# Mixing stage of a two-block transformer kernel: all transfers but weights and gate vectors issued from the GpSimd queue, gate columns by way of DRAM, head states and decay rows loaded ahead of the projections

## The chip, the cores and the metric

The kernel runs on one core of one Trainium2 chip. The metric is the time that the device takes for one execution, in microseconds, lower being better. A profile of one execution gives the rows that are read below. PE is TensorE (matrix products), DVE is VectorE, ACT is ScalarE, POOL is GpSimd, SP is SyncE, whose queue issues transfers and computes nothing. A name such as L1314 is line 1314 of the kernel before.

## The reference

Two transformer blocks are computed in float32 for one sequence of 512 tokens of width 1024. The first block has a feed-forward layer, a mixing layer and a second feed-forward layer, and beside the 512 tokens a context of 256 tokens goes through the first two. The second block (attention, cross attention to a memory, a feed-forward layer with a convolution) isn't touched here. The mixing layer is what matters:

```python
qk = silu(short_conv(concatenate([q, k]), conv_w, conv_b))      # q, k, v: 4 heads of 256
# for both directions (forward, reverse), per chunk of 128 tokens, per head:
b = cumsum(lf); g = b[-1]; w = g - b + li                        # lf: log forget gate, li: log input gate
m_new = maximum(g + m_st, max(w)); ws = exp(w - m_new); decay = exp(g + m_st - m_new)
c_new = decay * c_st + einsum('sv,sk->vk', v * ws, k)            # the state, passed to the next chunk
dm = b[t] - b[s] + li[s];  m_t = maximum(b + m_st, max(dm))
s_ts = (q @ k.T) * exp(dm - m_t)                                 # only s <= t
inter = exp(b + m_st - m_t)
h = (s_ts @ v + inter * (c_st @ q)) / maximum(|den|, exp(-m_t))
# the context's scan gives only the state that the 512 tokens start from
y_a = sigmoid(o) * head_layernorm(h_fwd + h_rev)
y_b = gelu(u) * spatial_mix(rmsnorm(gelu(vs)))
mixed = sigmoid(ga) * (y_a @ w_a) + sigmoid(gb) * (y_b @ w_b)
out = h + gate * (mixed @ w_out)
```

## The kernel before, in words

**Products.** Every float32 product is made of three: both operands are split into a high and a low part, and `mm3` (L109 to L111) adds high x high, high x low and low x high in one PSUM bank. Weights come in panels of 512 KB: `raw` (L94) loads one into one of three buffers from SP's queue, and `split` (L98 on ACT, L99 on DVE) makes the two parts. `fm` runs a panel against x: 24 products.

**Order.** The program is written once in a plain order. When the kernel is built, a planner lays the instructions of each engine into that engine's queue: what stands earlier in the program goes first, if by the planner's own estimates it is ready at that time; if not, something later is put there. On the chip each queue is then worked off strictly in order. So an instruction that becomes ready later than was estimated holds up everything behind it on its engine. A transfer also stands in the queue of the engine that issues it, and waits there for its source and its destination.

**The mixing stage** (`mix`, L1027) runs through these parts:
- the context's feed-forward layer; with it the norm of the 512 tokens, whose h is stored to DRAM (L1038);
- `lat_in`: gates and the last head's v for the 512 tokens (`cols_in`, v to DRAM at L1213); then `sgu`, whose u loop also makes the context's gates (`ctx_in`);
- the gate chain (`ctx_prep`, `lat_prep`): the gates as rows [4 heads, tokens], moved with small transfers (L1248, L1249), running sums by scans on DVE (L1253, L1266), exponentials on ACT; `decay_bc` (L1299, L1301) spreads the chunk decays over all partitions by way of DRAM; the rows dI and dM go to DRAM (L1338, L1339); `cols` stacks rows in one SBUF tile (L1311) and PE turns them into columns (L1314);
- the z loop, written behind the gate chain: 8 blocks, each the product of a gate panel with x and of a panel of w_branch_b with y_b;
- the context heads (`ctx_state`, 4 times): k and v of the head with the context's x, k turned token-major (`token_major`, L1395), for both directions two chunks of `state_update`, and the state to DRAM (L1430);
- the latent heads (4 times): `head_proj` makes k, q, v and o; `head_core` turns k, loads the states (L1440), makes the scores q k (L1445), loads for each direction a dM row (L1450, into a shared temporary) and a dI row (L1452), each spread over 128 partitions, forms P by a subtraction, a minimum, an exponential and a product with the scores (L1455 to L1460) and a triangular select on POOL (L1462); then 4 chunks in both directions with products with the state (L1476) and of P with v (L1477), state updates, and, where both directions of a chunk are there, a layer norm whose reciprocal root is on POOL (L1494) and whose turned output (L1503) is put off;
- the ga loop (gates to DRAM, L1067), the fin loop (gates back, L1075; L1082 loads h again), and the output product.

The last head's v isn't projected but loaded (L1360). Temporaries (`tmp`) share five buffers. All transfers of this stage but the first few small ones go out from SP's queue, between the weight panels. POOL does memsets, the small steps of the norms, the selects and the reciprocal roots.

Of the kernel before, what the change touches and what calls it, by code (L numbers as in the profile page):

```python
# [9 lines left out]
F32 = mybir.dt.float32  # L10
# [4 lines left out]
P = 128  # L15
D = 1024
KD = D // P
S = 512
# [7 lines left out]
class Core:  # L26
    def __init__(self, ctx, tc):
# [20 lines left out]
        nc.vector.tensor_copy(self.ones, one)  # L48
        self.mhalf = self.const.tile([P, 1], F32, name="mhalf")
# [7 lines left out]
    def flush(self, keep=0):  # L57
        """issues what was put off (but the last `keep`) so that products in between hide its wait"""
        while len(self.late) > keep:
            self.late.pop(0)()  # L60
# [23 lines left out]
    def spare(self, src, k):  # L84
        """like raw, in the space that the gate takes later"""
# [47 lines left out]
    def mean(self, ss, n, add=EPS, tag="s1"):  # L133
        """ss / n + add"""
# [4 lines left out]
    def power(self, m):  # L139
        """m ** -0.5"""  # L140
        rs = self.small()
        self.nc.gpsimd.tensor_tensor(out=rs, in0=m, in1=self.mhalf, op=ALU.pow)
        return rs
# [16 lines left out]
    def norm_tile(self, src, rs, A, B, out, t, banks=None):  # L160
        """src: the two halves [128 tok, 512]; out (hi, lo) [128, 8, N]; columns t*128.. are written."""
# [6 lines left out]
    def norm_steps(self, src, A, B, out, ts, step=None):  # L168
        """steps that norm the token tiles ts; src(t) gives the two halves."""
# [39 lines left out]
    def ranges(self, items, x, ranges, at=1):  # L209
        """items: (weights, psum); all of one token range come before the next range. What was put off is issued  # L210
        within the first range, after item `at`."""
# [5 lines left out]
    def ffn_pair(self, fs, w_in, x, ranges, n=S, w=None):  # L217
        """The two products of the tiles fs."""
# [13 lines left out]
    def ffn_in(self, pool, w_in, x, start, each, finish, w0=None):  # L232
        """start: tiles taken together while the last token tiles of x are still on their way."""
# [11 lines left out]
    def tm_out(self, act, w, kt, evac, post=None, ts=range(NT), tail=0, tail0=0, bk=range(NT), first=0):  # L245
        """act: list of (hi, lo) [128, 512] per contraction tile; w [kt*128, 1024]; evac(t, half, psum).
        In the second half the last panels are taken token tile by token tile, so post(t, half) can follow early."""
# [27 lines left out]
    def gate(self, i):  # L275
        """gate i with the vector along every row"""
# [31 lines left out]
def body(ctx, tc, a, out):  # L308
# [14 lines left out]
    with tc.tile_pool(name="start", bufs=1) as stp:  # L323
        def ada_pe(v, hf, parts):
            """steps for half a vector, one weight panel each. parts: 1: weights and conditions as they are;
            2: both as hi and lo."""
# [116 lines left out]
    def ada_dve(v, srcs):  # L443
        """queues the products for one vector; each piece is one weight panel. The sum over partitions: within
        blocks of 32 by transposes on DVE, then over the four blocks by a product that puts them in place."""
# [10 lines left out]
        def along_rows(hf, st):  # L456
            """the sums over partitions, on every row"""
# [97 lines left out]
def norm_post(K, h, A, B, g=None, bk=range(NT), store=None):  # L555
    """post(t, half) for tm_out: the norm of h as hi and lo. With g, h is first replaced by rmsnorm(h, g), and goes to `store`."""
# [50 lines left out]
def attention(K, a, h_d, cC, x, km_d, vm_d):  # L607
# [5 lines left out]
    with ExitStack() as sc:  # L613
# [7 lines left out]
        def queries(off, early=()):  # L621
            """the four panels of columns that start at off, for all tokens"""
# [8 lines left out]
        def proj_v(v, off, extra=None):  # L631
            """extra: [128, 4, n] for the n columns of w_in that follow v"""
# [12 lines left out]
        def proj_fox():  # L645
            """q has the high and the low part of a head in the two halves of the partitions, k the high part in both"""
# [22 lines left out]
        def pv(p, n, dst, copy=nc.vector.tensor_copy):  # L669
            """dst: per 128-block of p the (out, rhs, start, stop) of its product."""  # L670
# [9 lines left out]
        def pipeline(items):  # L680
            """items: generators; a stage of one item is issued together with earlier stages of the next ones."""
# [160 lines left out]
def memory_kv(K, a, src, rs, g, pool, km_d, vm_d, banks):  # L842
    """the keys and values of the memory, to DRAM; returns its steps, one weight panel each."""
# [31 lines left out]
def memory_attention(K, a, h, cC, x, km_d, vm_d, mp):  # L875
# [6 lines left out]
    def load(hd):  # L882
        """the head's keys and values"""
# [6 lines left out]
    def parts(hd):  # L890
        """the same in two parts each"""
# [22 lines left out]
    def weights(hd):  # L914
        """softmax over the memory for all tokens"""
# [113 lines left out]
def mix(K, a, h, xc, mods, affine, g_mix, g_head, g_sgu, g_ffn2, conv_w, conv_b):  # L1029
    nc, tc = K.nc, K.tc  # L1030
    w_in = a["w_in"][0]
    with ExitStack() as sc:
# [5 lines left out]
        K.bg.append(lambda: nc.sync.dma_start(out=hd_, in_=h))  # L1038
# [4 lines left out]
        with ExitStack() as sx:  # L1043
# [9 lines left out]
            with tc.tile_pool(name="ck", bufs=1) as ck:  # L1053
                for hd in range(NH):
# [503 lines left out]
```

## Time and profile before

| what | value |
|---|---|
| median of 3 runs | 2528.09 us (2526.84 to 2533.28) |
| span of the profiled execution | 2527.8 us |
| PE busy | 2451.1 us, 97% |
| DVE busy | 1358.2 us, 54% |
| ACT busy | 1012.5 us, 40% |
| POOL busy | 120.4 us, 5% |
| mean granted PE clock | 0.987 |
| share of 16 DMA engines' time, SP's queue | 43.3% |
| transfers issued by POOL | none |

The profiled execution's own time is its span, 2527.8 us from the first to the last instruction; no other time lies around it in the figures here, and it is 0.3 us under the median. Busy time is the union of an engine's instructions. Products on PE overlap, so PE can be busy and yet run at half the clock; the clock is read from the column PEclk, where 1.00 is 2.4 GHz and 0.50 is 1.2 GHz.

### The profile page before, as it was taken

To read this page: it belongs to the slowest core of one execution; us is meant where nothing else is said; L and a number is where in the kernel's file an instruction comes from. 1 tells how busy PE (TensorE), PEld (TensorE's weight loads), DVE (VectorE), ACT (ScalarE), POOL (GpSimd) and SP (SyncE) were. 2 spreads that over 40 slices of the span, in tenths; PEclk is the share of its full clock that TensorE was granted. 3 is DMA by queue.
4 is the path that set the end of the run, shared out by engine and by line. 5 is a ranking of instruction groups with operands and counts; after the bars stand their busy time and mean duration, and the time that the engine had idled before them with its cause. 6 is when DMAs were issued, how large, how long until landed. Compare 5 with 4: busy or idle time off the path is not lost.

```text
span 2527.8 us, 32182 instructions
## 1 busy us (share of the span) xinstructions
PE 2451.1 (97%) x12538; PEld 2040.3 (81%) x12538; DVE 1358.2 (54%) x2106; ACT 1012.5 (40%) x1685; POOL 120.4 (5%) x261
## 2 busy tenths in 40 slices
PE   8999999999999899999899999999999999999998
PEld 5778888899887688887688888888777788888887
DVE  5778755465445355566545333235485464666632
ACT  5533232354354344344234322224475453544422
POOL 2000000000010000000001000001020100000000
PEclk9999999999999999999999999999999999999999
DMA  8667654565754475454443333223213231333221
GB/s 266 218 188 218 181 167 159 171 185 185 172 81 97 78 138 138 79 87 78 84 161 111 108 98 94 100 92 110 75 29 106 76 117 50 107 95 101 94 99 67
DMA packets 373498, 307.09 MB, mean 121 GB/s; under 512 B 10579, under 2 KB 311043, under 8 KB 372833
## 3 DMA queue, kind: packets, MB, share of 16 engines
q1 hardware_dynamic: 371201, 301.35, 43.3%
q10 hardware_dynamic: 2144, 3.67, 0.4%
q8 instruction: 99, 1.62, 0.3%
q14 instruction: 54, 0.44, 0.1%
HBM read 291.43 MB, written 13.44 MB: 121 GB/s over the span
## 4 chain that ended last, share of the span: by engine, by line
PE 83%; DMA 6%; DVE 4%; issue 4%; ACT 2%; POOL 1%; SPq 0%; POOLq 0%; ACTq 0%; DVEq 0%
PE p L109 25%; PE p L110 25%; PE p L111 25%; DMA raw<-in_w_in_dram 2%; DMA tmp<-dM 2%; PE p L678 1%; DVE wl L99 1%; PE p L198 1%; ACT wh L98 1%; DMA gtmp<-gtmp 1%; PE p L673 1%; PE p L747 1%; PE p L1476 1%; PE p L1477 1%; DMA raw<-in_w_mkv_dram 0%
## 5 line engine op out<-in xcount | busy, mean ns | idle before, releaser
L99 DVE TENSOR_TENSOR wl<-raw,wh 128x1024 fp32r<-128x1024 f32 (+2 forms) x447 | 543.6, 1218 | 714.6 <-ACT wh L98 692.3
L98 ACT CAST wh<-raw 128x1024 fp32r<-128x1024 f32 (+2 forms) x447 | 466.7, 1046 | 942.1 <-PE p L110 371.9
L109 PE MATMUL p<-xh,wh 128*128 128x512 f32 (+1 forms) x1728 | 609.8, 353 | 3.8 <-ACT wh L98 2.3
L110 PE MATMUL p<-xl,wh 128*128 128x512 f32 (+1 forms) x1728 | 608.7, 353 | 0.6 <-DVE xl L207 0.6
L111 PE MATMUL p<-xh,wl 128*128 128x512 f32 (+1 forms) x1728 | 608.3, 352 | 0.0
L109 PEld LDWEIGHTS p<-xh,wh 128*128 128x128 f32 x1728 | 326.6, 189 | 48.9 <-ACT wh L98 2.7
L110 PEld LDWEIGHTS p<-xl,wh 128*128 128x128 f32 x1728 | 327.0, 189 | 45.2 <-DVE xl L207 1.0
L111 PEld LDWEIGHTS p<-xh,wl 128*128 128x128 f32 x1728 | 326.8, 189 | 43.9
L109 PE MATMUL p<-wh,ah 128*128 128x512 f32 x616 | 243.2, 395 | 0.5 <-ACT ah L98 0.5
L111 PE MATMUL p<-wh,al 128*128 128x512 f32 x616 | 242.7, 394 | 0.3 <-DVE al L99 0.3
L110 PE MATMUL p<-wl,ah 128*128 128x512 f32 x616 | 242.7, 394 | 0.0
L110 PE MATMUL p<-mxl,wh 128*128 128x512 f32 x384 | 155.9, 406 | 0.0
L111 PE MATMUL p<-mxh,wl 128*128 128x512 f32 x384 | 155.0, 404 | 0.0
L109 PE MATMUL p<-mxh,wh 128*128 128x512 f32 x384 | 154.6, 403 | 0.0
L111 PEld LDWEIGHTS p<-wh,al 128*128 128x128 f32 x616 | 115.9, 188 | 27.6 <-DVE al L99 0.8
L109 PEld LDWEIGHTS p<-wh,ah 128*128 128x128 f32 x616 | 116.0, 188 | 26.6 <-ACT ah L98 0.9
L110 PEld LDWEIGHTS p<-wl,ah 128*128 128x128 f32 x616 | 116.0, 188 | 25.5
L229 DVE TENSOR_TENSOR tmp<-tmp,p 128x512 f32<-128x512 f32 (+1 forms) x66 | 39.4, 597 | 96.4 <-PE p L111 94.4
L111 PEld LDWEIGHTS p<-mxh,wl 128*128 128x128 f32 x384 | 73.7, 192 | 16.8
L110 PEld LDWEIGHTS p<-mxl,wh 128*128 128x128 f32 x384 | 74.2, 193 | 15.8
L109 PEld LDWEIGHTS p<-mxh,wh 128*128 128x128 f32 x384 | 73.8, 192 | 15.8
L98 ACT CAST ah<-tmp 128x512 fp32r<-128x512 f32 (+1 forms) x88 | 49.8, 566 | 84.3 <-DVE tmp L1004 55.8
(422 smaller groups left out, 3578.6 us busy)
## 6 DMA issues: line engine op xcount, KB each, us to landing
raw<-in_w_ffn_in_dram SPq DMA_DIRECT2D x132, 512.0 KB
raw<-in_w_in_dram SPq DMA_DIRECT2D x98, 512.0 KB
raw<-in_w_ffn_out_dram SPq DMA_DIRECT2D x66, 512.0 KB
raw<-in_w_ada_dram SPq DMA_DIRECT2D x53, 512.0 KB
raw<-in_w_up_dram SPq DMA_DIRECT2D x44, 512.0 KB
raw<-in_w_down_dram SPq DMA_DIRECT2D x22, 512.0 KB
raw<-in_w_mkv_dram SPq DMA_DIRECT2D x16, 512.0 KB
raw<-in_w_out_dram SPq DMA_DIRECT2D x16, 512.0 KB
```

The lines of the kernel that those rows point to most:

```text
L98: self.nc.scalar.copy(hi, src)
L99: self.nc.vector.tensor_tensor(out=lo, in0=src, in1=hi.bitcast(F32), op=ALU.subtract)
L109: mm(out, ah, bh, start=start, stop=False)
L110: mm(out, ah, bl, start=False, stop=False)
L111: mm(out, al, bh, start=False, stop=stop)
L198: nc.tensor.transpose(ps[:, k * P:(k + 1) * P], hn[:, k * P:(k + 1) * P], self.ident)
L229: nc.vector.tensor_tensor(out=pr, in0=sa, in1=b, op=ALU.mult)
L673: nc.tensor.transpose(pt[:, j * P:(j + 1) * P], p[:, j * P:(j + 1) * P], K.ident)
L678: nc.tensor.matmul(out, pT[:, j * P:(j + 1) * P], rhs, start=start, stop=stop)
L747: nc.tensor.matmul(ps[:, b * L:(b + 1) * L], sq[p0:p0 + DH, c, i * P:L], sk[p0:p0 + DH, c, :L], start=True, stop=True)
L1476: nc.tensor.matmul(X, qi[:, j], C[d][:, j], start=j == 0, stop=False)
L1477: nc.tensor.matmul(X, Pm[d][:, c], T["v"][:, c, :HD + 1], start=False, stop=True)
```

## The change

`K.side_dma` is the issue of a transfer from POOL. In the mixing stage every transfer except weight panels, the gate vector and a few small loads of other queues now uses it. `stack` writes the gate rows to DRAM instead of one SBUF tile; `cols` loads them from there, and is called later in the program: the context's columns behind the first context head's k and v, the latent ones behind the last context state. `ctx_state` is split: `ctx_kv` of the next head stands ahead of the state updates of this one. `head_loads`, called first in `head_proj`, loads both states, both dM rows and both dI rows of a head; the dM tile (one buffer for each direction) is worked on in place until it is P. No arithmetic is added or left out. Doc strings are also dropped (not shown).

```diff
@@ class Core
+        self.side_dma = nc.gpsimd.dma_start
@@ mix
-        K.bg.append(lambda: nc.sync.dma_start(out=hd_, in_=h))
+        K.bg.append(lambda: K.side_dma(out=hd_, in_=h))
...
             with tc.tile_pool(name="ck", bufs=1) as ck:
+                kv = ctx_kv(K, ck, 0, xg, w_in, conv_w, conv_b, v_d[1])
+                G.ctx_cols()
                 for hd in range(NH):
-                    ctx_state(K, ck, hd, xg, w_in, conv_w, conv_b, G, C_d, v_d[1])
+                    nxt = ctx_kv(K, ck, hd + 1, xg, w_in, conv_w, conv_b, v_d[1]) if hd + 1 < NH else None
+                    ctx_state(K, ck, hd, kv, G, C_d)
+                    kv = nxt
+                G.lat_cols()
...
-                T = head_proj(K, hp, hd, x, w_in, conv_w, conv_b, v_d[0])
+                T = head_proj(K, hp, hd, x, w_in, conv_w, conv_b, v_d[0], G, C_d)
...
-                nc.sync.dma_start(out=ga_d[:, d], in_=ga)
+                K.side_dma(out=ga_d[:, d], in_=ga)
...
-                nc.sync.dma_start(out=ga, in_=ga_d[:, d])
+                K.side_dma(out=ga, in_=ga_d[:, d])
...
-            nc.sync.dma_start(out=h, in_=hd_)
+            K.side_dma(out=h, in_=hd_)
@@ class Gates
-            nc.sync.dma_start(out=v_d[:, t], in_=v)
+            K.side_dma(out=v_d[:, t], in_=v)
...
-            nc.sync.dma_start(out=LI, in_=g[8 * d:8 * d + 4, :])
-            nc.sync.dma_start(out=LF, in_=lf[8 * d + 4:8 * d + 8, :])
+            K.side_dma(out=LI, in_=g[8 * d:8 * d + 4, :])
+            K.side_dma(out=LF, in_=lf[8 * d + 4:8 * d + 8, :])
...
-            nc.sync.dma_start(out=dd[4 * d:4 * d + 4, :], in_=res[d]["decay"])
+            K.side_dma(out=dd[4 * d:4 * d + 4, :], in_=res[d]["decay"])
...
+    def ctx_cols(self):
+        self.ccols = self.cols(self.cstack, 2, "ctx")
+
+    def lat_cols(self):
+        self.lcols = self.cols(self.lstack, 4, "lat")
+
+    def stack(self, stacks, nch, name):
+        K = self.K
         n = nch * P
         r = len(stacks) * 4
-        st = self.tmp()[:r, :n]
+        st = K.dram.tile([r, n], F32, name=name + "_stack")
         for i, s in enumerate(stacks):
-            nc.sync.dma_start(out=st[4 * i:4 * i + 4, :], in_=s)
+            K.side_dma(out=st[4 * i:4 * i + 4, :], in_=s)
+        return st
+
+    def cols(self, st, nch, name):
+        K, nc = self.K, self.K.nc
+        r = st.shape[0]
+        rows = K.tmp()[:r, :nch * P]
+        K.side_dma(out=rows, in_=st)
+        st = rows
         ps = K.psB()
...
-        self.ccols = self.cols([res[0]["w"], res[1]["w"]], 2, "ctx")
+        self.cstack = self.stack([res[0]["w"], res[1]["w"]], 2, "ctx")
...
-            nc.sync.dma_start(out=self.dI[d], in_=it)
-            nc.sync.dma_start(out=self.dM[d], in_=r["M"])
+            K.side_dma(out=self.dI[d], in_=it)
+            K.side_dma(out=self.dM[d], in_=r["M"])
...
-        self.lcols = self.cols([res[0]["g"], res[1]["g"], res[0]["w"], res[1]["w"], floor[0], floor[1]], 4, "lat")
+        self.lstack = self.stack([res[0]["g"], res[1]["g"], res[0]["w"], res[1]["w"], floor[0], floor[1]], 4, "lat")
@@ head_v
-        nc.sync.dma_start(out=dst[:, :, 0:HD], in_=v_d)
+        K.side_dma(out=dst[:, :, 0:HD], in_=v_d)
@@ new, and head_proj
+def head_loads(K, hp, hd, G, C_d, T):
+    T["C"], T["mb"], T["ib"] = [], [], []
+    for d in range(2):
+        t = hp.tile([P, 2, HD + 1], F32, tag=f"C{d}", name="C", bufs=2)
+        K.side_dma(out=t.rearrange("p a b -> p (a b)"), in_=C_d[hd, d])
+        T["C"].append(t)
+        for n, src in (("mb", G.dM), ("ib", G.dI)):
+            t = hp.tile([P, S], F32, tag=f"{n}{d}", name=n)
+            K.side_dma(out=t, in_=src[d, hd].rearrange("(o n) -> o n", o=1).to_broadcast([P, S]))
+            T[n].append(t)
+
-def head_proj(K, hp, hd, x, w_in, conv_w, conv_b, v_d):
+def head_proj(K, hp, hd, x, w_in, conv_w, conv_b, v_d, G, C_d):
     nc = K.nc
     T = {}
+    head_loads(K, hp, hd, G, C_d, T)
@@ ctx_state
-def ctx_state(K, ck, hd, x, w_in, conv_w, conv_b, G, C_d, v_d):
-    nc = K.nc
+def ctx_kv(K, ck, hd, x, w_in, conv_w, conv_b, v_d):
     k = ck.tile([P, 2, NC], F32, tag="k", name="kc", bufs=2)
...
+    return k, v
+
+
+def ctx_state(K, ck, hd, kv, G, C_d):
+    k, v = kv
...
-        nc.sync.dma_start(out=C_d[hd, d], in_=C.rearrange("p a b -> p (a b)"))
+        K.side_dma(out=C_d[hd, d], in_=C.rearrange("p a b -> p (a b)"))
@@ head_core
-    C = []
-    for d in range(2):
-        t = hp.tile([P, 2, HD + 1], F32, tag=f"C{d}", name="C", bufs=2)
-        nc.sync.dma_start(out=t.rearrange("p a b -> p (a b)"), in_=C_d[hd, d])
-        C.append(t)
+    C, mbs, ib = (T[n] for n in ("C", "mb", "ib"))
...
-        mb = K.tmp()
-        nc.sync.dma_start(out=mb, in_=G.dM[d, hd].rearrange("(o n) -> o n", o=1).to_broadcast([P, S]))
-        t = hp.tile([P, S], F32, tag=f"ib{d}", name="ib")
-        nc.sync.dma_start(out=t, in_=G.dI[d, hd].rearrange("(o n) -> o n", o=1).to_broadcast([P, S]))
-        ib.append(t)
-        e = K.tmp().rearrange("p (c t) -> p c t", c=4)
+        pm = e = mbs[d].rearrange("p (c t) -> p c t", c=4)
         nc.vector.tensor_tensor(out=e, in0=G.lcols[:, :, 4 * d + hd:4 * d + hd + 1].to_broadcast([P, 4, P]),
-                                in1=mb.rearrange("p (c t) -> p c t", c=4), op=ALU.subtract)
+                                in1=e, op=ALU.subtract)
...
-        pm = hp.tile([P, 4, P], F32, tag=f"P{d}", name="P")
```

## Rows read from the trace of the kernel before

**Rows 1.** The page, busy time, share of the span and instructions of PE.
```profile
PE 2451.1 (97%) x12538; PEld 2040.3 (81%) x12538; DVE 1358.2 (54%) x2106; ACT 1012.5 (40%) x1685; POOL 120.4 (5%) x261
```
**Rows 2.** Busy time by stretch: engines in us, PEclk, DMA share, GB/s.
```profile
core 0: us, PE busy (x) PEld busy (x) DVE busy (x) ACT busy (x) POOL busy (x), PEclk, DMA share, GB/s
905.00:965.00 60.00, 54.17 (x386) 50.60 (x385) 41.36 (x77) 27.85 (x48) 0.20 (x2) 0.94 0.73 147
1151.00:1162.00 11.00, 7.48 (x25) 5.83 (x24) 6.63 (x16) 3.28 (x6) 1.39 (x2) 0.69 0.22 47
785.00:1250.00 465.00, 424.89 (x2241) 358.26 (x2240) 261.92 (x583) 184.10 (x280) 16.70 (x36) 0.95 0.51 95
```
**Rows 3.** What PE waited for from 785 to 1250: total us, times, longest.
```profile
PE p L1314 <- DMA gtmp<-gtmp: 14.7, 2, 10.6
PE p L1477 <- POOL P L1462: 13.1, 3, 8.6
PE p L1395 <- ACT kc L1353: 3.7, 2, 2.0
PE p L109 <- DVE kT L99: 2.3, 1, 2.3
PE p L109 <- ACT kTc L98: 2.1, 2, 1.8
...
PE p L1476 <- DVE kT L99: 1.9, 1, 1.9
```
**Rows 4.** Busy time by stretch, six stretches behind stalls of PE.
```profile
807.00:813.00 6.00, 6.00 (x16) 4.72 (x17) 1.89 (x3) 0.00 (x0) 0.51 (x1) 0.50 0.33 92
849.60:853.90 4.30, 4.30 (x13) 3.48 (x14) 0.26 (x1) 0.00 (x0) 0.15 (x2) 0.50 0.65 99
940.70:946.00 5.30, 4.94 (x22) 4.65 (x23) 3.77 (x5) 3.42 (x6) 0.00 (x0) 0.50 0.83 178
1007.60:1010.90 3.30, 3.30 (x11) 2.65 (x11) 2.46 (x7) 0.51 (x1) 1.23 (x2) 0.50 0.64 79
...
1155.30:1161.10 5.80, 5.80 (x15) 4.76 (x16) 3.62 (x10) 1.93 (x4) 0.63 (x1) 0.50 0.24 50
1220.30:1225.90 5.60, 5.60 (x15) 4.57 (x16) 3.61 (x10) 1.95 (x4) 0.63 (x1) 0.50 0.22 32
```
**Rows 5.** Timeline of PE, z loop: start us, length us, line, operation.
```profile
809.88 0.63 PE L109 MATMUL p<-ybh,wh 128*128 128x512 f32 x1
810.31 0.63 PE L110 MATMUL p<-ybl,wh 128*128 128x512 f32 x1
810.74 0.63 PE L111 MATMUL p<-ybh,wl 128*128 128x512 f32 x1
...
819.21 0.40 PE L110 MATMUL p<-ybl,wh 128*128 128x512 f32 x1
819.44 0.39 PE L111 MATMUL p<-ybh,wl 128*128 128x512 f32 x1
```
**Rows 6.** The chain of waits from 780 to 1260: start us, us, what.
```profile
934.57 8.28 DMA raw<-in_w_in_dram
...
995.96 8.21 DMA raw<-in_w_in_dram
...
1202.70 14.12 DMA tmp<-dM
```
**Rows 7.** Timeline of SP's queue, context heads and first latent head.
```profile
926.75 6.63 SPq L1430 DMA_DIRECT2D c_store<-Cc  x1
...
981.51 2.98 SPq L1450 DMA_DIRECT2D tmp<-dM  x1
```
**Rows 8.** Timeline of PE, first context head.
```profile
904.29 0.60 PE L1395 MATMUL p<-ident,kc 128*128 128x128 f32 x4
904.64 0.36 PE L109 MATMUL p<-mch,wh 128*128 128x256 f32 x1
```
**Rows 9.** Timeline of POOL, first selects of two latent heads [idle before <-releaser].
```profile
1085.58 0.76 POOL L1462 TENSOR_SCALAR_AFFINE_SELECT P<-P 128x512 f32<-128x512 f32 x1 [51.74 <-DVE P L1460]
...
1219.52 0.70 POOL L1462 TENSOR_SCALAR_AFFINE_SELECT P<-P 128x512 f32<-128x512 f32 x1 [36.45 <-DVE P L1460]
```
**Rows 10.** All instructions with the tensor dM: ns min/median/max, first and last start.
```profile
L1450 SPq DMA_DIRECT2D tmp<-dM x8: 572/2485/4760, 977.6 to 1203.4; - x8
```

More of the change, by code (lines that the diff above doesn't have):

```diff
@@ L1298, in decay_bc @@
         for d in range(2):
-            nc.sync.dma_start(out=dd[4 * d:4 * d + 4, :], in_=res[d]["decay"])
+            K.side_dma(out=dd[4 * d:4 * d + 4, :], in_=res[d]["decay"])
         t = self.pool.tile([P, 8, nch], F32, name=name + "_decay")
-        nc.sync.dma_start(out=t.rearrange("p a b -> p (a b)"), in_=dd.rearrange("a b -> (a b)").rearrange("(o n) -> o n", o=1).to_broadcast([P, 8 * nch]))
+        K.side_dma(out=t.rearrange("p a b -> p (a b)"), in_=dd.rearrange("a b -> (a b)").rearrange("(o n) -> o n", o=1).to_broadcast([P, 8 * nch]))
         return t
-    def cols(self, stacks, nch, name):
-        K, nc = self.K, self.K.nc
+    def ctx_cols(self):
[4 more added lines that the diff above has]
+        K = self.K
         n = nch * P
         r = len(stacks) * 4
-        st = self.tmp()[:r, :n]
+        st = K.dram.tile([r, n], F32, name=name + "_stack")
         for i, s in enumerate(stacks):
-            nc.sync.dma_start(out=st[4 * i:4 * i + 4, :], in_=s)
+            K.side_dma(out=st[4 * i:4 * i + 4, :], in_=s)
[6 more added lines that the diff above has]
+        st = rows
         ps = K.psB()
@@ L1446, in head_core @@
     K.flush()
-    Pm, ib = [], []
+    Pm = []
     for d in range(2):
-        mb = K.tmp()
-        nc.sync.dma_start(out=mb, in_=G.dM[d, hd].rearrange("(o n) -> o n", o=1).to_broadcast([P, S]))
-        t = hp.tile([P, S], F32, tag=f"ib{d}", name="ib")
-        nc.sync.dma_start(out=t, in_=G.dI[d, hd].rearrange("(o n) -> o n", o=1).to_broadcast([P, S]))
-        ib.append(t)
-        e = K.tmp().rearrange("p (c t) -> p c t", c=4)
+        pm = e = mbs[d].rearrange("p (c t) -> p c t", c=4)
         nc.vector.tensor_tensor(out=e, in0=G.lcols[:, :, 4 * d + hd:4 * d + hd + 1].to_broadcast([P, 4, P]),
-                                in1=mb.rearrange("p (c t) -> p c t", c=4), op=ALU.subtract)
+                                in1=e, op=ALU.subtract)
         nc.vector.tensor_scalar(out=e, in0=e, scalar1=0.0, scalar2=None, op0=ALU.min)
         nc.scalar.activation(e, e, AF.Exp)
-        pm = hp.tile([P, 4, P], F32, tag=f"P{d}", name="P")
         nc.vector.scalar_tensor_tensor(out=pm, in0=sps.rearrange("p (c t) -> p c t", c=4), scalar=1.0 / 16.0, in1=e, op0=ALU.mult, op1=ALU.mult)
```

## Prediction, made before the result was known

> **What bounds the kernel now.** I read the page first, then the waits of TensorE (PE), then PE's busy time by stage, and only then the queues. PE is busy 97% of the profiled span [rows 1], so time can be won only where PE stands still or runs slowly. The mixing stage that the change touches holds its gate columns, context heads and latent heads between 785 and 1250 us. There PE is busy 424.89 of 465 us [rows 2], 40.1 us idle; before and after it (the z, branch and output products) I see no wait of PE worth naming, so I cost everything outside at nothing.
>
> The waits of PE in that stretch [rows 3] name the idle time almost wholly: 14.7 us for the gate columns (L1314), 13.1 us for the decay-weighted scores P (L1477), 3.7 us for the context keys (L1395), 2.3 and 1.9 us for latent work, 2.1 us for the context key splits. Behind the longer of them the granted clock stands at 0.50, which is 1.2 GHz instead of 2.4: [rows 4] are the stretches right behind six stalls in which PE is busy at that clock, 6.00, 4.30, 4.94, 3.30, 5.80 and 5.60 us. At full clock one 512-column product starts 0.23 us after the last (819.21, 819.44), at half clock 0.43 us (810.31, 810.74) [rows 5]. So a microsecond of work at half clock gives back 1 - 0.23/0.43 = 0.465 us when the stall before it goes.
>
> Then what is late behind each wait. SP issues weights and everything else in one queue. The chain of waits [rows 6] shows one weight panel landing 8.28 us after its issue, another 8.21 us after, and the last head's dM row 14.12 us after. SP's own row [rows 7]: one store of the context state holds SP for 6.63 us at 926.75 while it waits for VectorE, and the panel that PE then needs goes out only at 934.57 [rows 6]; a dM load holds it 2.98 us at 981.51, and the panel behind it goes out at 995.96 [rows 6].
>
> **The change, part by part.** 84 transfers leave SP's queue for POOL's: 1 store and 1 load of h, 8 stores and 8 loads of the ga gates, 8 and 8 of the context states, 8 dM and 8 dI rows, 6 stores and 2 loads of v, and 26 small gate transfers. Two loads are new (the stacked gate rows come back from DRAM), so POOL issues 86. No product, split or activation is added or removed; PE's work stays the same.
>
> *Gate columns.* Their transposes now stand behind the first context head's products, and behind the last context state. With all of SP's delays PE had both columns' rows by 849.60 [rows 4], and the first context head's products end at 904.29, where its transposes start [rows 8]. So the stores and the load that replace the old transfers have some 50 us of products to hide under. On POOL the transfers stand between the gate chain's own memsets (L1257), which only this chain waits for. Gone: 14.7 us idle [rows 3] and (6.00 + 4.30) x 0.465 = 4.8 us of slow clock [rows 4]: **19.5 us**. Without that cover, two loads would cost about what the two stalls cost now.
>
> *Context heads.* Stores of the state no longer stand before weight panels, and the next head's keys and values are given ahead of the state updates. Order alone gives little: the trace already has products with the context's x straight behind a head's transposes [rows 8], which are the next head's. It is the panel of 934.57 that counts: 3.7 us for L1395 plus 2.1 - 1.8 = 0.3 us of the key splits, and 4.94 x 0.465 = 2.3 us: **6.3 us**. The other 1.8 us I leave in: DMA engines are busy 0.73 of 905 to 965 [rows 2], and a panel may still come late.
>
> *First latent head.* PE waited 2.3 us for a key split that stood on VectorE behind the split of the panel of 995.96. With dM off SP this panel goes out earlier: 2.3 + 3.30 x 0.465 = **3.8 us**.
>
> *Decay rows ahead of the projections.* Each head's two C, two dM and two dI loads go out before its four projections. dM has one buffer for each direction, now reused in place as P, so a load waits until PE has used the previous head's P. POOL's rows [rows 9] show the room: it idles 51.74 and 36.45 us between a head's last reciprocal root and the next head's first select (three such rows), against a landing of at most 14.12 us [rows 6]. So the subtraction, minimum and exponential can be done while projections run, and P needs only its product and its select (0.76 and 0.70 us on POOL [rows 9]). Gone: 13.1 us and (5.80 + 5.60) x 0.465 = 5.3 us: **18.4 us**. The 1.9 us of L1476 is a wait for a split on VectorE [rows 3], and stays.
>
> *The remaining transfers* (h, ga, v): PE shows no stall at their places, the cover is the running products; zero. SP is also freed there, but weights are not late there; zero again.
>
> Sum of gains: 19.5 + 6.3 + 3.8 + 18.4 = 48.0 us.
>
> **New costs.** No transfer from POOL is in the trace. For its price on POOL I bound by SP's own issues of the same dM row: 0.57 us at the least, 4.76 us at the most, median 2.49 [rows 10]. The long ones stood behind weight panels in one ring; POOL's queue has none, so I take 0.6 us. A queue is in order: up to four loads (2 dM, 2 dI) of heads 1 to 3 can stand before the last reciprocal roots of the head that ends (L1494), for which its layer norm and then PE's last transposes (L1503) wait. 3 x 4 x 0.6 = 7 us at the most, half of it felt: 4 us; at 4.76 us it would be 57 us. Select behind sooner products: the short wait of about 1 us that head 1 shows (13.1 in three, of which 8.6 the longest [rows 3] and 11.00 - 7.48 = 3.5 the next [rows 2]) may come twice: 2 us, from 0 to 4. The gate columns' loads: 2 us, from 0 to the 14.7 they cost now. Together 8 us. By the Trainium skill, page "DMA: Bandwidth & Descriptors", section "Latency and other measured facts", the first byte of a transfer issued by GpSimd takes about 1 us where SP's takes 0.6; no run here shows it yet. An estimate from that page makes 3 x 4 x 1.0, half felt, 6 us instead of 4, and the sum 2490 us.
>
> **Sum.** 2527.8 - 48.0 + 8 = 2487.8, so **2488 us**. The span and the median of the runs (2528.09) differ by 0.01%, and I make no correction for it.
>
> **Rivals.**
> *Every head stalls as head 0 does.* Once P is early, the order may put its products close behind the scores, and PE waits for splits and selects in each head: 3.8 us, as before 1007.60. Then that term stays and three more come: 2488 + 3.8 + 3 x 3.8 = 2503 us. For it: PE's order is fixed at build time from estimates, and head 0 is the one with dM already there. Against it: that wait came from a late panel, not from P.
> *The loads aren't ahead after all.* One buffer for dM, and POOL's queue may hold the load behind a step that waits; the 18.4 us stay: 2506 us. Against it stand the 36 us of room.
> *POOL's queue becomes the wait* (the other side). Place: end of heads 0 to 2, four loads before the last roots. Price: 12 loads by their issue, all felt. It eats the net gain of 44 us (48 less the 4 of the other new costs) at 3.7 us each, and beyond that the kernel is slower: at 5 us, 2528 - 44 + 60 = 2544 us. For it: one issue of 4.76 us on SP [rows 10]. Against it: median 2.49 us in a full ring, and POOL is busy 16.70 of the 465 us [rows 2]. On the page "SBUF — State Buffer" the Trainium skill says, in "Who interferes with whom", that a transfer issued from GpSimd is starved while VectorE holds the port pair that the two share, and advises SP or ACT for it; this speaks against the change. No run here shows it; if it held, this rival is where it would be seen.
>
> **How the numbers follow.** Forecast 0.70, between 2474 and 2501; head stalls 0.12; loads not ahead 0.05; POOL's queue 0.09, split into 0.01 faster, 0.03 no change and 0.05 slower; 0.04 for an order at build time that is worse in a way I can't name, all slower. Less than 0.3% (7.6 us) either way is about what this measurement can't tell from no change. Of the first three cases, 0.87, I move 0.05 to no change and 0.02 to slower, since unknown POOL prices touch all of them. Faster: 0.80 + 0.01 = 0.81; no change 0.03 + 0.05 = 0.08; slower 0.05 + 0.04 + 0.02 = 0.11. The lower end is every idle and slow microsecond of the stretch gone, 40.1 us, 29.94 of slow work [rows 4] x 0.465 = 13.9, and 1.5 more as an estimate for slow work behind the 1.9 us wait (as long as the one behind the first latent head's): 55.5, so 2472. The upper end takes in the two middle rivals with POOL's issues at SP's median, 12 x 2.49 = 30 instead of 4: 2488 + 26 = 2514, and a little of the head stalls: 2518 us.
>
> **What would show it.** Right: no wait of PE for L1314 beyond 1 us; VectorE's wait for dM at L1455 gone; L1477 waits below 1 us; SP's rows between 785 and 1250 hold weight panels alone; PE's idle time there about 14 us instead of 40, and no clock of 0.50 behind the former stalls. Wrong: PE waits at L1503 behind POOL's L1494, or POOL rows in which a transfer takes several us; a column transpose waiting for its load behind a context store on POOL; weight panels landing as late as now, because the engines and not SP's queue held them.

## The result, and the profile after

The changed kernel takes 2499.13 us (median of 4 runs, 2497.02 to 2500.8) against 2527.53 us for the one before: a ratio of 0.9888, 95% interval 0.9872 to 0.9905. It is faster by 28.4 us, inside the range, near the upper end of 2474 to 2501, and 11 us short of the forecast of 2488. The profiled execution took 2496.0 us, 31.8 less than that of before. A line of the kernel has moved by 1 before the gate columns and by 21 to 39 behind them, but for the load of dM, which now stands earlier: L1314 is now L1335, L1395 L1430, L1430 L1469, L1450 L1401, L1462 L1491, L1476 L1505, L1477 L1506, L1503 L1532.

The page after, against [rows 1]:

```profile
PE 2437.1 (98%) x12538; PEld 2030.3 (81%) x12538; DVE 1352.7 (54%) x2106; ACT 1011.8 (41%) x1685; POOL 167.3 (7%) x347
```

PE has the same instructions and 14.0 us less busy time (less of it at half clock); POOL has 86 instructions more. To see where the 31.8 us came from I cut both executions at 785 us and then at the same work: the end of the last z product, the last state update of the context heads (last product with kTc), and the first product with y_a. Busy time in these four stretches, before:

```profile
785.00:893.00 108.00, 93.29 (x389) 75.32 (x388) 42.89 (x75) 38.60 (x52) 1.78 (x6) 0.92 0.46 84
893.00:962.70 69.70, 63.87 (x476) 60.74 (x476) 46.37 (x81) 36.07 (x60) 0.20 (x2) 0.95 0.74 146
962.70:1276.70 314.00, 294.44 (x1495) 243.83 (x1494) 178.79 (x433) 116.90 (x179) 14.71 (x28) 0.96 0.48 93
1276.70:2527.80 1251.10, 1231.70 (x6136) 1019.13 (x6134) 613.07 (x868) 502.28 (x897) 68.51 (x149) 1.00 0.30 94
```

and after:

```profile
785.00:875.20 90.20, 90.20 (x402) 73.77 (x401) 43.48 (x74) 40.67 (x54) 15.44 (x33) 1.00 0.54 98
875.20:950.60 75.40, 63.92 (x481) 60.58 (x480) 46.40 (x84) 35.49 (x60) 5.33 (x11) 0.95 0.71 143
950.60:1241.90 291.30, 284.70 (x1495) 237.91 (x1494) 174.29 (x432) 117.65 (x179) 33.91 (x62) 1.00 0.51 100
1241.90:2496.00 1254.10, 1232.46 (x6136) 1018.94 (x6134) 613.10 (x868) 502.28 (x897) 72.82 (x158) 1.00 0.30 94
```

The gate chain and the z loop lose 17.8 us by this cut, and PE stands still there no more. But 785 us isn't the same work in both. The products that turn the gates into rows, where the gate chain starts, come 2.7 us later in the execution after, before and after:

```profile
783.50 0.60 PE L1220 MATMUL p<-ident,lat_gc 128*16 128x128 f32 x4
```
```profile
786.23 0.60 PE L1226 MATMUL p<-ident,lat_gc 128*16 128x128 f32 x4
```

From there on the stretch loses 20.5 us. The 2.7 us ahead of it lie within the spread between executions: the kernel with the loads ahead alone (below), whose products are the same as before up to there, gets there 3.0 us later. The latent heads and the ga loop lose 22.7 us. The context heads, in between, take 5.7 us **longer**: 11.5 us of PE's time is idle where 5.8 was. The rest is 3.0 us longer, nearly all of it at the end of the program. The last store of the result goes out 3.8 us before the end of the span in the kernel before (2527.8) and 6.7 us in the one after (2496.0):

```profile
2524.06 0.38 SPq L1020 DMA_DIRECT2D out_dram<-h  x1
```
```profile
2489.32 0.38 SPq L1021 DMA_DIRECT2D out_dram<-h  x1
```

What comes last is a DRAIN in POOL's queue, a step at the program's end that computes nothing. It takes 7.7 us instead of 0.7. All 11 profiles of kernels that issue these transfers from POOL have it so long (7.5 to 7.7), the other three don't (0.7).

PE's waits after, 785 to 1250, against [rows 3]:

```profile
PE p L110 <- ACT kTc L99: 9.3, 3, 5.6
PE p L1505 <- DVE kT L100: 2.6, 1, 2.6
PE p L1532 <- DVE tmp L1527: 1.9, 5, 0.5
PE p L1532 <- DVE s L1510: 1.9, 2, 1.3
...
```

No gate columns, no P; what is left of weight is the split of the context's keys on ACT. ACT's timeline shows what stands before that split [idle before <-releaser]:

```profile
923.95 1.04 ACT L99 CAST wh<-raw 128x1024 fp32r<-128x1024 f32 x1 [1.21 <-DMA raw<-in_w_in_dram]
924.90 0.58 ACT L99 CAST kTc<-p 128x512 fp32r<-128x512 f32 x1
```

A panel's split, waiting for its load, comes first in ACT's queue. And the chain of waits shows how long panels take to land around there:

```profile
902.86 14.87 DMA raw<-in_w_in_dram
...
920.14 12.56 DMA raw<-in_w_in_dram
```

That is no later than before. [rows 6] shows 8.28 and 8.21 us, but the same chain of the kernel before has, ahead of these, another panel issued during the context heads, which I passed over:

```profile
917.65 14.51 DMA raw<-in_w_in_dram
```

SP no longer holds them: where [rows 7] had a store of 6.63 us, its timeline now has panels alone for 324.80 us. The other transfers are on POOL's timeline, each 0.5 to 0.8 us, with the first selects behind them:

```profile
854.49 324.80 SPq L95 DMA_DIRECT2D raw<-in_w_in_dram  x51
```
```profile
956.33 0.54 POOL L1401 DMA_DIRECT2D mb<-dM  x1
...
993.39 1.24 POOL L1491 TENSOR_SCALAR_AFFINE_SELECT mb<-mb 128x512 f32<-128x512 f32 x2 [33.19 <-DVE mb L1489]
...
1008.62 0.55 POOL L1401 DMA_DIRECT2D mb<-dM  x1
```

### The profile page after: what moved, and what is told of

Same layout as the page of the kernel before. It is cut to its first block, busy times and chain, and to the rows that moved or that the text cites. A ratio compares the mean times of both kernels' runs of the same rounds, so it can differ in the third digit from the quotient of the medians.

```text
span 2496.0 us, 32238 instructions
## 1 busy us (share of the span) xinstructions
PE 2437.1 (98%) x12538; PEld 2030.3 (81%) x12538; DVE 1352.7 (54%) x2106; ACT 1011.8 (41%) x1685; POOL 167.3 (7%) x347
## 4 chain that ended last, share of the span: by engine, by line
PE 82%; DMA 7%; issue 4%; DVE 4%; ACT 2%; POOL 1%; POOLq 0%; ACTq 0%; SPq 0%; DVEq 0%
PE p L110 25%; PE p L112 25%; PE p L111 25%; DMA raw<-in_w_in_dram 4%; DMA raw<-in_w_ffn_in_dram 2%; DVE wl L100 1%; PE p L679 1%; ACT wh L99 1%; PE p L199 1%; PE p L1505 1%; PE p L674 1%; PE p L748 1%; PE p L342 1%; PE p L1506 0%; PE p L715 0%
```

## The experiments

Two theories for the 11.5 idle us. **A**: the weight panels of the context heads land too late, whatever the order. **B**: with the next head's keys and values given ahead, the splits of its panels stand before this head's key splits on ACT and VectorE, and the state updates wait for a panel that they don't need. The expectations speak of a stage from the last z product to the first latent product (59.6 us before, 60.7 after); the table uses the longer cut of above, up to the last state update, since orders differ in what they put behind the first latent product. Ratios are to the kernel before, run beside it on the same chip (there its medians were 2530.5 to 2531.9 for all rows from the third on); the changed kernel again, beside the others, shows how far its own figures move.

| kernel | median us | ratio (95%) | context heads, us | PE idle in it | then to y_a, us |
|---|---|---|---|---|---|
| before | 2527.53 | | 69.7 | 5.8 | 314.0 |
| after | 2499.13 | 0.9888 (0.9872 to 0.9905) | 75.4 | 11.5 | 291.3 |
| after, again | 2500.65 | 0.9888 (0.9875 to 0.9902) | 76.2 | 11.8 | 293.8 |
| heads in turn | 2499.66 | 0.9876 (0.9854 to 0.9898) | 68.6 | 5.4 | 295.0 |
| SP's queue | 2496.51 | 0.9867 (0.9847 to 0.9887) | 78.0 | 11.4 | 290.3 |
| POOL's queue alone | 2525.86 | 0.9986 (0.9972 to 1.0) | 73.8 | 8.5 | 294.4 |
| loads ahead alone | 2511.58 | 0.9921 (0.9908 to 0.9935) | 75.5 | 8.8 | 290.0 |
| wide key panels | 2495.88 | 0.9859 (0.9839 to 0.9879) | 68.7 | 4.7 | 295.1 |
| wide, in turn | 2499.05 | 0.9871 (0.9858 to 0.9885) | 67.5 | 3.9 | 295.4 |
| first columns twice | 2507.94 | 0.9917 (0.9903 to 0.9931) | 81.7 | 16.1 | 292.7 |
| second columns twice | 2500.72 | 0.9880 (0.9860 to 0.9900) | 73.0 | 7.9 | 291.9 |
| head 3 first | 2497.94 | 0.9869 (0.9850 to 0.9888) | 69.3 | 5.8 | 297.2 |
| head 3 first, wide | 2498.09 | 0.9868 (0.9850 to 0.9886) | 68.9 | 6.2 | 297.2 |
| half the loads | 2489.01 | 0.9827 (0.9812 to 0.9842) | 62.0 | 0.1 | 294.0 |

**Which part gave the gain.** The changed kernel from SP's queue:

```diff
-        self.side_dma = nc.gpsimd.dma_start
+        self.side_dma = nc.sync.dma_start
```

> The changed kernel with its side transfers from SP's queue in place of GpSimd's; order, loads ahead and the stacked columns as they are. If the earlier issue alone made the gain: head loads come ahead of the projections, so they wait for little, and the time stays within 4 us of 2499. If the other queue was needed (a store that waits for its data holds up all weight panels behind it on SP, as the state stores of 6 us did before): stalls of 5 to 15 us come back at the context head stores and the rows of the gates, 2510 to 2520.

It is no slower. The state store holds SP again (7.01 us at 908.77) and the context's columns wait, as PE's waits show, yet the time doesn't tell it from the kernel from POOL's queue. Some 3 us of what SP's queue costs there it gets back at the end of the program, where its last store is issued 3.2 us before the end and not 6.7:

```profile
PE p L110 <- ACT kTc L99: 6.7, 2, 6.5
PE p L1335 <- DMA tmp<-ctx_stack: 4.2, 1, 4.2
```

The kernel before, with the same transfers from POOL:

```diff
...
-        nc.sync.dma_start(out=C_d[hd, d], in_=C.rearrange("p a b -> p (a b)"))
+        nc.gpsimd.dma_start(out=C_d[hd, d], in_=C.rearrange("p a b -> p (a b)"))
...
```

> The kernel before with the same transfers of the mixing stage from GpSimd's queue, nothing else. If SP's order was the cause of the stalls, the loads of the decay rows no longer stand between panels: the waits for panels go (some 5 us at 785 to 1250 and the 8 us panel after 995), but the column rows and the decay rows of the first head still arrive as late as they are asked for, so 2512 to 2522 against 2527.5. If the queue alone is enough: 2500. If GpSimd's issue is dear (over 3.7 us for each): slower than 2527.

No gain that can be told from none. In its profile the wait for P is gone and the stretch to y_a is as short as after (294.4 us), so the rows of dM come in time from a queue without panels too; but the gate columns wait longer than in [rows 3]:

```profile
PE p L1314 <- DMA gtmp<-gtmp: 21.8, 2, 16.6
PE p L1395 <- ACT kc L1353: 8.1, 3, 3.0
```

The stretch up to the last z product takes 117.7 us instead of 108.0, of which 3.1 us lie ahead of the gate chain. POOL's queue alone gives back there (6.5 us) and in the context heads (4.1) more than half of the 19.6 us that it gains. Where the rest goes this profile doesn't say: its execution was 8 us slower than the median, and took 1261.3 us behind y_a instead of 1251.1. The loads ahead alone, on SP, in the kernel before:

```diff
 def head_proj(...):
     ...
     T = {}
+    head_loads(K, hp, hd, G, C_d, T)
     ...
```

> The kernel before, in which only the states and decay rows of a latent head are loaded ahead of its projections, from SP's queue; column transposes and order of the context heads as before. By the prediction's terms this is the decay rows (18.4) and the first head's load of states (about 1.5), so 20 us less: 2508 against 2528, no wait for the rows left at the latent heads, and 267 to 270 us in place of 287 from 963 to 1250. Rival: on SP the first head's loads wait for the last state store and hold up the panels behind them by 6 to 12 us, so only 8 to 14 us are gained, 2514 to 2520.

2511.58, some 20 us less, as forecast for the term of the decay rows. That the sum fits so well is in part luck: the stretch to y_a loses 24.0 us, more than forecast, and the context heads give 5.8 back. The rival's stalls are there too (a store holds SP 6.55 us at 929.17, the context heads take 75.5 us), only not in the heads that gain; the gate columns wait as before (14.1 us).

**Order or panels.** The changed kernel with the heads in turn:

```diff
-                kv = ctx_kv(K, ck, 0, ...)
-                G.ctx_cols()
                 for hd in range(NH):
-                    nxt = ctx_kv(K, ck, hd + 1, ...) if hd + 1 < NH else None
+                    kv = ctx_kv(K, ck, hd, ...)
+                    if hd == 0:
+                        G.ctx_cols()
                     ctx_state(K, ck, hd, kv, G, C_d)
-                    kv = nxt
```

> The changed kernel with one part undone: each context head's keys and values are again followed at once by its own state updates. Theory A (the weight panels of the context stage land too late, whatever the order): TensorE stands still there about as long as in the changed kernel (11.5 us between 785 and 951), and the time stays within 3 us of 2499. Theory B (the next head's panel splits stand ahead of this head's key splits on ScalarE and VectorE, so the state updates wait for a panel they don't need): the idle time falls to 6 us or less, as in the kernel before, and the time to some 2492 to 2494. Prediction's own step: the stage gets longer by the waits for keys of 1 to 3 us in three heads, so 4 to 6 us slower, 2503 to 2505.

The profile speaks for theory B (idle 5.4 us, heads 6.8 us shorter than after); the median does not (2499.66), and the stretch behind gives 3.7 us back. The profile is that of the fastest of five executions (2493.78). The prediction's own step, slower by 4 to 6 us, came out in neither. Wide key panels:

```diff
+    w = [K.panel(w_in, 512 * i, 4, O_K + hd * HD, HD) for i in range(2)]
     for j in range(2):
         ps = K.psA()
-        K.fm(ps, K.panel(w_in, 0, KD, O_K + hd * HD + j * P, P), x, 0, NC)
+        for kk in range(KD):
+            wh, wl = (t[:, kk % 4, j * P:(j + 1) * P] for t in w[kk // 4])
+            K.mm3(...)
```

> The changed kernel, with a context head's key panels taken as two panels of four row tiles by 256 columns (runs of 1 KB) in place of two of eight by 128 (runs of 512 bytes); same bytes, same products. Theory A (landing of panels): one panel (the last key panel of head 3) has packets of some 124 ns in place of 40, for its columns or for its short runs. If for its short runs, the wide panels land in 6 to 9 us and the idle time of the stage falls from 11.5 us to under 6, time 2492 to 2496; if all panels are late alike, or the columns are slow in any shape, no change (within 3 us of 2499). Theory B: no change, since the order of the splits stays; or slower by 1 to 2 us, since a product starts only when both panels are there.

Here the order of the splits is theory B's, and the heads are as short as in turn (68.7). Which of the two reasons it was, the expectation didn't foresee: idle time fell, yet packets of 1 KB at the place of the slow panel took 123 to 163 ns, so its columns are slow in this shape too. That other panels came sooner instead is only argued. Both edits together, and the changed kernel again:

> The changed kernel with both edits tried so far: wide key panels of the context heads, and each head's keys and values followed at once by its own state updates. Alone they gave stages of 54.9 and 57.6 us in place of 60.7. Theory A: the order is worth little by itself, the stage is 53 to 56 us, and the time 2492 to 2496. Theory B: both gains add up, the stage is some 52 us, and the time 2490 to 2493.

> The changed kernel itself once more, for a second profile and a time beside the other runs of this call: 2497 to 2501. If the stage of the context heads is again 60 us or more with 10 us or more idle, the difference to the order in turn (57.6 and 4.6) is more than the spread between two executions; if it comes out at 57 to 59, that difference says nothing.

The second profile has 11.8 us idle and heads of 76.2, so the 6 to 7 us of the profiles are more than their spread. With wide panels the order is worth only 1.2 us of the heads, so the gains don't add up, which is theory A's side; but the stage of 57.6 us and the median of 2499.05 are over what either expected.

**The slow panel.** Head 3's second key panel reads the first one's columns (half of that head's context keys then come from other weights); then the reverse:

```diff
-        K.fm(ps, K.panel(w_in, 0, KD, O_K + hd * HD + j * P, P), x, 0, NC)
+        K.fm(ps, K.panel(w_in, 0, KD, O_K + hd * HD + (0 if hd == NH - 1 else j) * P, P), x, 0, NC)
```

> The changed kernel, in which the second key panel of context head 3 reads the columns of the first one (so the second half of that head's context keys is computed from other weights); bytes, runs and order as they are. In every kernel so far one panel at this place has packets of 104 to 170 ns in place of some 40. Theory A: it is this panel's columns that are slow, and they make the longest stall of the stage: with other columns the packets near 900 to 912 take some 40 ns, the gap of 5.6 us before the state update goes, the stage (60.7 us from the last z product to the first latent product) falls to 52 to 55, and the time to 2491 to 2494. If it is the place in the program (two streams at once, whatever the columns): packets and stage stay as they are, 2499. Theory B: the wait moves little, since any panel split stands ahead of the key split: 58 to 60 us, 2497 to 2499.

> The counterpart of the kernel with other columns: both key panels of context head 3 read the columns of the second one (so the first half of that head's context keys is computed from other weights). With the first one's columns in both, the slow packets lasted twice as long (904 to 924), the longest stall was 12.8 us in place of 5.6 and 7.5, and the stage 67.8 us in place of 60.7 and 61.7. Theory A, with the panel now named (the first key panel of head 3 is the slow one): no packets over 100 ns from 895 to 930, no stall over 3 us, stage 52 to 55 us, time 2490 to 2494. Rival (both panels of that head are slow, or what lengthened the packets was reading one place twice): slow packets for 20 us again, stage 62 to 68, time 2500 to 2508.

The first was a miss that named the culprit: I had the wrong one of two panels, and now the slow one is loaded twice. The same 24 us in three kernels (share of the DMA engines' time and GB/s are the last two columns), after:

```profile
900.00:924.00 24.00, 15.74 (x127) 15.02 (x125) 13.08 (x23) 10.12 (x19) 1.23 (x3) 0.96 0.75 118
```

with the first columns twice, and with the second twice:

```profile
900.00:924.00 24.00, 17.88 (x134) 17.25 (x132) 10.30 (x20) 6.40 (x11) 1.22 (x3) 0.93 0.70 45
```
```profile
900.00:924.00 24.00, 18.05 (x131) 17.75 (x132) 14.77 (x24) 10.49 (x19) 1.23 (x3) 0.89 0.62 125
```

Columns 1792 to 1919 of w_in move at 45 GB/s with the engines busy 0.70 of the time. It is not the place in the program: latent head 3 loads the same columns again, by their order in SP's queue at 1091.80, and the kernel after then moves as little:

```profile
1094.00:1104.00 10.00, 10.00 (x58) 8.73 (x57) 5.91 (x8) 4.88 (x7) 0.00 (x0) 1.00 0.76 46
```

One copy costs 5.5 to 6.3 us more of heads (81.7 against 75.4 and 76.2) and some 7 to 9 us of time; without any, 2.4 to 3.2 us go, and no more: 7.9 us of idle time stay, so the expected 52 to 55 us was missed (58.2), and with it 2490 to 2494 us (2500.72). The slow panel is a part of the lateness, not all of it.

**Taking the slow panel first, and leaving loads out.** Order 3, 0, 1, 2:

```diff
-                kv = ctx_kv(K, ck, 0, ...)
+                order = (3, 0, 1, 2)
+                kv = ctx_kv(K, ck, 3, ...)
                 G.ctx_cols()
-                for hd in range(NH):
-                    nxt = ctx_kv(K, ck, hd + 1, ...) if hd + 1 < NH else None
+                for i, hd in enumerate(order):
+                    nxt = ctx_kv(K, ck, order[i + 1], ...) if i < 3 else None
```

> The changed kernel with the context heads in the order 3, 0, 1, 2, nothing else: the slow panel comes to the start of the stage, where its load is asked for some 20 us before its product. Theory A: its slow landing is hidden by that lead, the other 13 panels land at some 3.5 us each beside products that take longer, so idle time falls from 11 to 5 us or less, the stage to 52 to 56 us, and the time to 2491 to 2495. Rival (the lead is used up there, and the panels of the next heads come late instead): the same 8 to 11 us of idle time, earlier in the stage, 2498 to 2501.

> Head 3 first, and the key panels of the context heads wide (four row tiles by 256 columns) as in the run that gave a stage of 54.9 us. Theory A: the slow columns are then spread over two panels at the start; idle 4 us or less, stage 51 to 54 us, time 2489 to 2494. If the wide panels gained only through the slow one, it equals the run with head 3 first alone within 2 us.

The stage of the expectations is 55.4 and 53.1 us, as theory A said, and the heads are 6 to 7 us shorter than after, with a little more idle time (5.8 and 6.2 us up to the last state update) than was expected of the stage. In time little of it is left (2497.94 and 2498.09, over theory A's range): the stretch to y_a has grown from 291.3 and 293.8 to 297.2. The two times agree, which was to be expected if wide panels gain only through the slow columns. Last, half of the loads left out (7 of 14 panels, and half of these weights are then others):

```diff
+    w = K.twice(w_in, 0, KD, O_K + hd * HD, P)      # one load, split twice
     for j in range(2):
         ps = K.psA()
-        K.fm(ps, K.panel(w_in, 0, KD, O_K + hd * HD + j * P, P), x, 0, NC)
+        K.fm(ps, w[j], x, 0, NC)
...
```

> The changed kernel with half of the context heads' weight loads left out: each head loads its first key panel and its first value panel and splits each of them twice, the second time in place of the panel left out (7 of 14 loads of 512 KB go; splits, products, state updates and their order stay; half of the weights are then others). Theory A (the stage waits for the landing of its panels, in any order): the stage becomes as long as its products alone, 49 to 52 us in place of 60.7 and 61.7, with idle time of 2 us or less and no stretch at half clock. Theory B (the order of the splits on ScalarE and VectorE makes the state updates wait): the splits are all there in the same order, so the waits for kTc stay and the stage is 57 to 62 us. In time: 10 us of stage would make 2489 to 2491; the runs with a stage of 53 to 58 us came out at 2495.9 to 2500.7, so a part of it may be lost to the spread between executions or given back in the stage behind: 2488 to 2496.

The stage is 48.1 us. Its windows up to the last state update, and all that PE waits for between 785 and 1250 above 1 us:

```profile
785.00:876.30 91.30, 91.30 (x406) 74.65 (x406) 43.41 (x74) 40.57 (x54) 15.50 (x33) 1.00 0.53 94
876.30:938.30 62.00, 61.91 (x480) 58.98 (x480) 46.27 (x84) 36.15 (x60) 5.35 (x11) 1.00 0.60 119
```
```profile
PE p L1515 <- DVE kT L100: 2.6, 1, 2.6
PE p L1542 <- DVE tmp L1537: 2.6, 6, 0.6
PE p L1542 <- DVE s L1520: 2.1, 2, 1.6
```

0.1 us idle, clock 1.00, no wait for kTc, with every split in place and in theory B's order. Time: 2489.01, 10 to 12 us less. Theory A holds: the stage waits for panels. Theory B is half of a cause: the order alone costs nothing, but while panels are late it decides what else has to wait for them.

## Why the prediction came out as it did

*Gate columns*: right. Forecast 19.5 less 2 of new costs; measured from the start of the gate chain 20.5, so the 2 us of new costs didn't come. The wait is gone, no load waits behind a state store. By the runs with one queue alone, it is the later place of the transposes that does it, not POOL: POOL alone made this wait 7.1 us longer.

*Decay rows ahead, and the first latent head*: right in size. Forecast 18.4 + 3.8 = 22.2, measured 22.7 for the stretch of both (20.2 in the second profile), and 20 in time for the loads ahead alone. The reason given for the 3.8 us was not shown: behind the dM load at 981.51 SP waited 11.4 us for VectorE to split an earlier panel, and only then sent the panel of 995.96. What I didn't see is that the rows had two cures: from POOL, without any load ahead, they come in time as well.

*Context heads*: this step failed. It said that a store holds SP, that the panel of 934.57 [rows 6] is therefore late, and that 6.3 us go with the store; and that "order alone gives little". SP is free of the store now, and the panels land as late as before (14.87 and 12.56 us; before, 14.51). Not SP's queue but the loads themselves hold them: the DMA engines are 0.74 busy in this stretch before and 0.71 after, and without half of the loads the waits are gone. Panels that land as late as before are the last of the signs that the prediction named for being wrong. Instead of 6.3 us less the stretch takes 5.7 more, a difference of 12.0 us. The signs I had in hand: DMA engines 0.73 busy in this stretch and 0.51 in the mean [rows 2], and a panel that took 14.51 us; I left 1.8 us of waits in for it, where 11.5 came. And the order, held to be worth little, cost 6.8 to 7.6 us of this stretch in the profiles: with the heads in turn and SP as free it takes 68.6 us, 1.1 less than before, which is all that is left of the 6.3.

*New costs of 8 us*: too high, which covered most of that miss by luck. POOL's issues were priced right (0.54 against 0.6 us), but the 6 us behind selects and roots didn't come: the latent stretch lost all that was forecast gross. A cost that it put at nothing did come: 2.9 us at the end of the program, where POOL's queue takes 7.7 us for its last DRAIN. Sum: -40.0 forecast; +12.0 context heads, -6.5 costs behind the latent heads and what they gained beyond the forecast, -3.0 columns, +3.0 behind y_a, nearly all of it that DRAIN, +2.7 ahead of the gate chain, the spread between executions: -31.8.

*Rivals.* P's product waits in no head; 2.6 us at L1505 (1.9 were forecast to stay) and 3.8 us at L1532 are left. The loads were ahead, but VectorE's wait for dM is not gone, as the prediction had it: 6.5 us in four waits, where 24.0 in five were; PE waits for none of them. POOL's queue did not become the wait: VectorE waits 4.8 us in all for POOL's roots, and no select starts late:

```profile
DVE tmp L1527 <- POOL s L1523: 4.8, 11, 0.8
```

The Trainium skill, page "SBUF — State Buffer", section "Who interferes with whom", says that a transfer which VectorE seems to stall was issued by GpSimd, starved of the port time for its descriptors, and it names the two-port modes of VectorE in which that happens. The trace does not show it here, nor how much of VectorE's time is in those modes: with VectorE busy 54% of the span, the profile's list of issues gives a median of 3.9 us to landing for the eight dM loads from POOL.

```profile
mb<-dM POOLq DMA_DIRECT2D x8, 256.0 KB, 3.9
```

What stays open: with the heads in turn the stretch waits 5.8 us in the kernel before and 5.4 without stores on SP, but 8.5 and 8.8 in the two kernels in which only one part was changed and the columns' stalls stayed (POOL's queue alone, loads ahead alone); no run says why. And of the 6 to 8 us that the shorter heads save in the profiles, 1 to 6 come back behind them, and what is left can't be told from the changed kernel: wide key panels (0.9859) is the fastest that computes the same, with an interval that overlaps. Nor is it shown what about the loads makes them late: the DMA engines' rate, or the three buffers, each of which comes free only when VectorE has split its panel. In the kernel after, from 875 to 951 us, SP has panels alone to issue and waits 28.3 us for such splits and 21.5 us for a load; leaving loads out relieves both, and no run has more buffers. The times are coarse partly for a reason outside the stage: in 5 of the 14 profiles (SP's queue, POOL's queue alone, wide in turn, head 3 first, half the loads) the granted clock stands at 0.50 for 10 us near 1790 or 1820 us and some 5 us are lost, in the others not.

## What to carry to other kernels

Before a stall is booked as gained, look at the stage behind it: here one in which the DMA engines were busy 0.74 of the time did not go faster for having its issuing queue freed, and an overlap that put the next panel's split ahead of this step's work handed late panels on to it. Read all of a chain's rows for such a stage, not the two that fit. Test the queue and the place of a transfer apart; here the place (loads ahead, transposes later) gave the gain, and the queue nothing that could be told in the time, with 3 us of cost at the program's end. To see whether a stage waits for loads or for order, leave out loads and keep everything else.

## What the runs showed of the hardware

Panels of one shape and one matrix move at rates that differ with their columns. The two key panels of head 3 are neighbours, and with the one or the other loaded twice the same 24 us moved 45 or 125 GB/s, at 0.70 and 0.62 of the engines' time; the latent head that loads the slow ones again moves 46 GB/s at 0.76, and a load of 256 columns that held them had packets of 123 to 163 ns. The Trainium skill, page "DMA: Bandwidth & Descriptors", section "Latency and other measured facts", has copies slow down at row pitches of large powers of two; all panels of w_in have one pitch, 32,832 bytes, so the pitch alone doesn't say which columns are slow, and no run here shows what does.

A kernel that issues transfers from POOL ends later. With 84 or 86 of them POOL's last DRAIN takes 7.5 to 7.7 us (11 profiles) instead of 0.7 (3 profiles), and the program ends 6.5 to 6.7 us after the issue of its last store instead of 3.2 to 3.9. What POOL does in that time the trace doesn't show.
